# One table set for exponential and logarithm in the gates of a two-layer encoder kernel, and the lower bounds ahead of the first head

## The chip, the cores and the metric

The kernel runs on one core of a Trainium2 chip. The metric is device time in microseconds (us) for one execution, the median of several. The engines are TensorE (PE, with its weight loads as PEld), VectorE (DVE), ScalarE (ACT), GpSimd (POOL) and SyncE (SP), which issues transfers.

## The reference

Two layers of a bidirectional encoder trunk over 512 positions and 1024 channels, in float32. In each layer three branches start from one normalized input; their results are gated, summed, projected and added to the residual, and an MLP follows. The change touches branch A, a gated linear recurrence with four heads of 128 channels, run forward and backward. Its gates need an exponential and a logarithm:

```python
def hgrn2_gate(z, lb):
    zf = z.astype(jnp.float32)
    log_f = jnp.logaddexp(jnp.log(lb), jnp.log1p(-lb) + jax.nn.log_sigmoid(zf))
    key = (1.0 - lb) * jax.nn.sigmoid(-zf)
    return log_f, key
...
    p = jax.nn.softmax(lb_logits.astype(jnp.float32), axis=0)
    cum = jnp.cumsum(p, axis=0)
    lower = (cum - cum[0:1]).reshape(DEPTH, 2, A_HEADS, A_KDIM)
...
    merged = (gates[:, :, 0] * (y_a @ w_br[l, 0])
              + gates[:, :, 1] * (y_b @ w_br[l, 1])
              + gates[:, :, 2] * (y_c @ w_br[l, 2]))
```

`lower` is zero in layer 0, so only layer 1 needs the lower bounds' values. Branch B is a gated mixing with GELUs (computed with tanh), branch C an attention over a window of 128 positions with a softmax (exponentials), and `gates` are sigmoids (computed with tanh).

## The kernel before

Activations lie with channels on the 128 partitions and the 512 positions along the free dimension, or the other way round where a product asks for it. Matrix products are made exact enough by splitting each float32 operand into a high and a low part: ScalarE writes the high part of a weight chunk (L201), VectorE the low part (L202), and TensorE multiplies three of the four combinations (L206 to L208 and the like). Weights stream in 512 KB chunks on SyncE's queue.

A layer runs in stages. First come the token-major projections and the outer merge gates (`seven`, `on_gate`, which end in a tanh at L859 or L865). Then comes the stage of the three branches, which holds the change. Then the output projections and the MLP, where neither exponential nor logarithm is used. A second, smaller norm and spill of the residual connect the layers.

In the branch stage the program text runs: `a_ffb(0)` (two gate projections `f`, scaled into `z2` at L782, then `a_gates`), the query `q`, and `a_head` for head 0. Then in layer 0 `lower_bounds`. Then branch B's GELUs and mixing, the attention's keys and values, and by turns attention groups (`c_run`: `c_scores` with its Exp at L1022 and L1024, transposes `pT` at L1044 copied at L1045, outputs `po` copied to `yc` at L1057), the heads 1 to 3 (`head`), and columns of branch B's merge (`merge_b`: projection `gz`, tanh at L947, product `mg` at L953). A scheduler reorders all of this when the program is built: it takes, per engine, what is ready by a model of the durations, by the order of the text and by priorities (`hp`, `later`). The result is a fixed queue for each engine. `behind(mark)` makes every instruction in its block queue after `mark` on that engine.

`a_gates` computes on ScalarE the absolute value of `z2` (L582), its Exp (L583) and the Ln of one plus that (L584); in layer 1 a second round follows for the lower bound: Abs (L596), Exp (L598), Ln (L599). `a_head` makes from the cumulative sums `ex` many Exps: the factors `qt` and `kt` (L631, L634) for six block lengths, `key` (L648), `dec` (L676, L677), `kd` and `qd` (L682, L699). TensorE transposes `kd` (L685), ScalarE copies the transpose `kT` (L687), and TensorE multiplies it with the values (`stp`, L690).

[...] The program builder follows the finished ScalarE queue and puts an ACT_TABLE_LOAD before each activation whose function the loaded set lacks. These loads carry the line of the activation they precede. A load can also be asked for by the set's name.

## Time and profile before

| | |
|---|---|
| median of 3 executions | 1664.61 us (1662.26 to 1665.77) |
| the profiled execution | 1664.05 us |
| its span, first to last instruction | 1662.3 us |
| TensorE busy | 1640.4 us, 99% |
| VectorE busy | 1364.2 us, 82% |
| ScalarE busy | 1024.6 us, 62% |
| mean granted TensorE clock | 0.997 |

A row of a group names the source line, the engine, the operation, the result and its operands with their shapes, the count and, after the bar, busy us and the mean ns of one. A row of the timeline gives start and duration in us, and in brackets how long the engine had been idle and which instruction ended that. A row of waits names who waited for whom, with total us, times and longest. A row by stage gives the stage, its length, the busy time of PE, PEld, DVE, ACT and POOL with instruction counts, the granted clock of TensorE (1.00 is full), the share of time that the transfer engines are busy, and GB/s.

### The profile page before, as it was taken

The numbers are of one execution on the slowest core, as the hardware profiler recorded it, in microseconds if no ns is written. First come the engines' busy times: TensorE is split into PE (matmuls) and PEld (weight loads), VectorE is DVE, ScalarE is ACT, GpSimd is POOL, SyncE is SP. The second block draws the span as 40 slices with busy tenths as digits, with TensorE's granted clock in tenths as the row PEclk, the third lists the DMA queues.
The fourth block names the chain that finished last, engine by engine and source line by source line (L and its number), as shares of the span: only waits on it lengthen the run. The fifth ranks groups of instructions, "written<-read, shape, count | busy, mean of one in ns | idle before, by whom it ended". The sixth has DMA issues, their size and how long they took to land.

```text
span 1662.3 us, 24318 instructions
## 1 busy us (share of the span) xinstructions
PE 1640.4 (99%) x9137; PEld 1377.5 (83%) x9137; DVE 1364.2 (82%) x2183; ACT 1024.6 (62%) x1743; POOL 100.2 (6%) x165
## 2 busy tenths in 40 slices
PE   8999999999999999999999999999999999999998
PEld 6878887888888898989878888888888888989896
DVE  7887987877667989888989869888776589888987
ACT  7566578776246555646666665887862474646474
POOL 0011000000300000000010110000003000000001
PEclk9999999999999999999999999999999999999999
DMA  8243221322725233332423432212226243332311
GB/s 306 102 152 124 77 79 69 102 77 96 247 95 191 75 116 107 110 102 102 140 89 115 152 113 83 89 71 77 96 96 234 102 178 102 102 116 88 127 64 51
DMA packets 55589, 191.54 MB, mean 115 GB/s; under 512 B 7376, under 2 KB 7632, under 8 KB 55472
## 3 DMA queue, kind: packets, MB, share of 16 engines
q1 hardware_dynamic: 44352, 154.43, 27.0%
q0 software_dynamic: 10688, 35.00, 5.7%
q8 instruction: 72, 1.18, 0.3%
q10 hardware_dynamic: 432, 0.55, 0.1%
q14 instruction: 45, 0.37, 0.1%
HBM read 173.18 MB, written 16.78 MB: 114 GB/s over the span
## 4 chain that ended last, share of the span: by engine, by line
PE 66%; DVE 3%; ACT 2%; issue 1%; POOLq 0%; ACTq 0%; DVEq 0%
PE up L206 4%; PE up L207 4%; PE up L208 4%; PE dA L430 3%; PE dA L431 3%; PE dA L429 3%; PE us L517 2%; PE us L519 2%; PE us L518 2%; PE dC L430 2%; PE dC L429 2%; PE dC L431 2%; PE wo L249 2%; PE wo L250 2%; PE wo L248 2%; PE gA L429 1%
## 5 line engine op out<-in xcount | busy, mean ns | idle before, releaser
L201 ACT CAST wh<-wq 128x1024 fp32r<-128x1024 f32 x214 | 225.3, 1053 | 224.2 <-PE dA L430 61.3
L202 DVE TENSOR_TENSOR wl<-wq,wh 128x1024 fp32r<-128x1024 f32 x214 | 259.8, 1219 | 67.3 <-ACT wh L201 63.2
L201 ACT CAST wh<-wr 128x1024 fp32r<-128x1024 f32 x165 | 172.9, 1048 | 150.9 <-PE wo L249 23.4
L202 DVE TENSOR_TENSOR wl<-wr,wh 128x1024 fp32r<-128x1024 f32 x165 | 201.0, 1219 | 68.7 <-ACT wh L201 61.1
L208 PE MATMUL up<-xh,wl 128*128 128x512 f32 x320 | 124.7, 390 | 0.0
L207 PE MATMUL up<-xl,wh 128*128 128x512 f32 x320 | 124.7, 390 | 0.0
L206 PE MATMUL up<-xh,wh 128*128 128x512 f32 x320 | 124.5, 391 | 0.0
L430 PE MATMUL dA<-wh,sh 128*128 128x512 f32 x256 | 99.7, 389 | 0.0
L429 PE MATMUL dA<-wh,sh 128*128 128x512 f32 x256 | 98.4, 390 | 0.0
L431 PE MATMUL dA<-wl,sh 128*128 128x512 f32 x256 | 91.8, 389 | 0.0
L643 DVE TENSOR_TENSOR ex<-ex 128x512 f32<-128x512 f32 x112 | 74.7, 683 | 0.3
L206 PEld LDWEIGHTS up<-xh,wh 128*128 128x128 f32 x320 | 60.1, 188 | 12.6 <-ACT wh L201 0.2
L208 PEld LDWEIGHTS up<-xh,wl 128*128 128x128 f32 x320 | 60.1, 188 | 12.4
L207 PEld LDWEIGHTS up<-xl,wh 128*128 128x128 f32 x320 | 60.1, 188 | 12.2
L631 ACT ACTIVATE qt<-ex 128x512 f32<-128x512 f32 x56 | 38.0, 678 | 35.4 <-DVE ex L643 34.2
L429 PEld LDWEIGHTS dA<-wh,sh 128*128 128x128 f32 x256 | 48.0, 188 | 10.0
L431 PEld LDWEIGHTS dA<-wl,sh 128*128 128x128 f32 x256 | 48.1, 188 | 9.9
L430 PEld LDWEIGHTS dA<-wh,sh 128*128 128x128 f32 x256 | 48.1, 188 | 9.9
L518 PE MATMUL us<-xs,wh 128*128 128x256 f32 x192 | 54.1, 283 | 0.0
L517 PE MATMUL us<-xs,wh 128*128 128x256 f32 x192 | 54.1, 283 | 0.0
L519 PE MATMUL us<-xs,wl 128*128 128x256 f32 x192 | 53.3, 283 | 0.0
L207 PE MATMUL gz<-xl,wh 128*128 128x512 f32 x128 | 51.0, 399 | 0.0
(431 smaller groups left out, 4792.8 us busy)
## 6 DMA issues: line engine op xcount, KB each, us to landing
wr<-in_ws_dram SPq DMA_DIRECT2D x159, 512.0 KB, 3.5
wq<-in_ws_dram SPq DMA_DIRECT2D x124, 512.0 KB, 4.3
thd<-zt POOLq DMA_DIRECT2D x32, 256.0 KB, 2.5
gt<-thd POOLq DMA_DIRECT2D x32, 256.0 KB, 4.3
mgd<-mg POOLq DMA_DIRECT2D x16, 256.0 KB, 2.5
mB<-mgd POOLq DMA_DIRECT2D x16, 256.0 KB, 6.3
x<-in_xT_dram SPq DMA_DIRECT2D x8, 256.0 KB, 6.5
xt<-in_xt_dram SPq DMA_DIRECT2D x8, 256.0 KB, 5.8
```

Of the source, the lines that this page charges most:

```text
L201: nc.scalar.copy(hi, raw)
L202: nc.vector.tensor_tensor(lo, raw, hi.bitcast(F32), ALU.subtract)
L206: nc.tensor.matmul(pt, whi, xhi, start=first, stop=False)
L207: nc.tensor.matmul(pt, whi, xlo, start=False, stop=False)
L208: nc.tensor.matmul(pt, wlo, xhi, start=False, stop=last)
L429: nc.tensor.matmul(pt, xh[:, t], hi[:, c], start=start and k == 0, stop=False, skip_group_check=True)
L430: nc.tensor.matmul(pt, xl[:, t], hi[:, c], start=False, stop=False, skip_group_check=True)
L431: nc.tensor.matmul(pt, xh[:, t], lo[:, c], start=False, stop=k == 3, skip_group_check=True)
L517: nc.tensor.matmul(pt, hi[:, c], xh, start=n in (1, 2, 7) and k == 0, stop=False, skip_group_check=True)
L518: nc.tensor.matmul(pt, hi[:, c], xl, start=False, stop=False, skip_group_check=True)
L519: nc.tensor.matmul(pt, lo[:, c], xh, start=False, stop=k == 3, skip_group_check=True)
L643: nc.vector.tensor_tensor(o_ap, o_ap, ap_of(ex, i_, [[istep, 2]] + z), ALU.add)
```

## The change

Layer 0's call of `lower_bounds` moves ahead of the gates of its first head. In `lower_bounds` and in `a_gates` a load of the set `natural_log_exp_and_others` is asked for by name, queued on ScalarE behind the last Exp that comes before a Ln. Layer 0's head 0 is left without such a load of its own. The second logarithm of layer 1's gates (L599) is not touched.

```diff
@@ lower_bounds
         nc.scalar.activation(ea, ea, AF.Exp)
-        nc.scalar.activation(eb, eb, AF.Exp)
+        with behind(nc.scalar.activation(eb, eb, AF.Exp)):
+            nc.scalar.preload_act_table_set("natural_log_exp_and_others")
         s = SM("lb", 8)
@@ before a_gates
+    def log(t, mark):
+
+        if mark:
+            with behind(mark):
+                nc.scalar.preload_act_table_set("natural_log_exp_and_others")
+        nc.scalar.activation(t, t, AF.Ln, bias=onep_t[:, 0:1])
+
@@ a_gates
         nc.scalar.activation(e, z2, AF.Abs)
-        nc.scalar.activation(e, e, AF.Exp, scale=-1.0)
-        nc.scalar.activation(e, e, AF.Ln, bias=onep_t[:, 0:1])
+        mark = nc.scalar.activation(e, e, AF.Exp, scale=-1.0)
+        log(e, mark if l or h else None)
@@ trunk, start of the branch stage
         oa = []
+        if l == 0:
+            lbs = lower_bounds()
         g0 = a_ffb(0)
         q0 = evac(proj(xs, "q", l, "q", 0), "q", "q")
         oa.append(a_head(l, 0, g0, q0, vt))
-        if l == 0:
-            lbs = lower_bounds()
```

## The prediction

> **What bounds the kernel now.** I read the page first: engine totals, then the chain that ended last.

> ```profile
> span 1662.3 us, 24318 instructions
> PE 1640.4 (99%) x9137; PEld 1377.5 (83%) x9137; DVE 1364.2 (82%) x2183; ACT 1024.6 (62%) x1743; POOL 100.2 (6%) x165
> PE 66%; DVE 3%; ACT 2%; issue 1%; POOLq 0%; ACTq 0%; DVEq 0%
> ```

> TensorE (PE) is busy for 1640.4 of 1662.3 us and carries nearly all of the chain that a line is named for. ScalarE (ACT), the only engine whose work the change cuts, is busy 62%. So time taken off ScalarE counts only where PE stands still, or runs slowly, because of ScalarE. PE's whole idle time is 1662.3 - 1640.4 = 21.9 us: a ceiling over start, end and all stages.

> The second view is PE's waits, for the two stretches in which branch A's heads run: 140 to 420 us (layer 0), then 965 to 1250 us (layer 1).

> ```profile
> PE stp L690 <- ACT kT L687: 1.4, 1, 1.4
> PE po L1055 <- ACT pT L1045: 0.4, 1, 0.4
> PE pT L1044 <- ACT yc L1057: 0.4, 1, 0.4
> ...
> PE kT L685 <- ACT kd L682: 2.2, 1, 2.2
> PE pT L1044 <- DVE es L1026: 1.1, 1, 1.1
> PE pT L1044 <- ACT yc L1057: 0.6, 1, 0.6
> ```

> Columns: who waited for whom, total us, times, longest. These six waits, 6.1 us together, are all the standing still that a quicker ScalarE queue could remove inside the heads. Five name ScalarE, and the sixth (es) hangs on a ScalarE Exp.

> Third, how many table loads there are and which line they stand before (ScalarE's groups with shapes kept apart; count, busy us, mean ns):

> ```profile
> L584 ACT ACT_TABLE_LOAD x8 | 10.3, 1283 | 0.1
> L631 ACT ACT_TABLE_LOAD x4 | 5.1, 1283 | 1.1 <-DVE lbd L573 1.0
> L599 ACT ACT_TABLE_LOAD x4 | 5.1, 1283 | 0.1
> L676 ACT ACT_TABLE_LOAD x3 | 3.8, 1283 | 0.1
> L568 ACT ACT_TABLE_LOAD x2 | 2.6, 1283 | 0.0
> ...
> L947 ACT ACT_TABLE_LOAD x1 | 1.3, 1283 | 0.0
> ...
> L598 ACT ACT_TABLE_LOAD x1 | 1.3, 1283 | 0.0
> ```

> The view has 29 loads of 1.283 us; the rows left out are the one at the start and five before exponentials (L1022, L1024, L682). Fourteen stand before a logarithm (L584, L599, L568), fourteen before the next exponential or tanh after one. So today a logarithm evicts the exponential's tables and the next exponential brings them back.

> Fourth, ScalarE's timeline where PE waited: layer 0 head 2, then layer 1 head 1, then head 2.

> ```profile
> 285.43 1.28 ACT L682 ACT_TABLE_LOAD   x1
> 286.72 0.52 ACT L682 ACTIVATE kd<-ex 128x384 f32<-128x384 f32 x1
> ...
> 1049.91 1.28 ACT L676 ACT_TABLE_LOAD   x1
> 1051.31 0.51 ACT L682 ACTIVATE kd<-ex 128x384 f32<-128x384 f32 x1
> 1059.64 0.61 ACT L947 ACTIVATE gz<-gz 128x512 f32<-128x512 f32 x1
> 1061.87 1.28 ACT L599 ACT_TABLE_LOAD   x1
> 1064.84 1.28 ACT L1024 ACT_TABLE_LOAD   x1
> ...
> 1107.15 1.28 ACT L676 ACT_TABLE_LOAD   x1
> 1122.35 1.28 ACT L1024 ACT_TABLE_LOAD   x1
> ```

> In each, a load that brings the exponential back runs a microsecond or two before the instruction that PE waits for. PE's rows beside them, and the granted clock there:

> ```profile
> 288.07 0.94 PE L690 MATMUL stp<-vt,kT 128*128 128x128 f32 x6 [1.43 <-ACT kT L687]
> 1051.87 0.55 PE L685 MATMUL kT<-id_t,kd 128*128 128x128 f32 x3 [2.16 <-ACT kd L682]
> 1053.05 0.63 PE L207 MATMUL gz<-xl,wh 128*128 128x512 f32 x1
> ...
> 1125.59 0.52 PE L1044 MATMUL pT<-id_t,sc 128*128 128x128 f32 x3 [1.06 <-DVE es L1026]
> 286.00:292.00 6.00, 4.16 (x25) 3.00 (x24) 4.31 (x9) 5.90 (x14) 0.00 (x0) 1.00 0.00 0
> 1052.00:1057.00 5.00, 5.00 (x18) 4.19 (x19) 4.28 (x12) 4.94 (x16) 0.00 (x0) 0.66 0.30 108
> ```

> In the two last rows the figure behind the engines' busy times is the granted clock. After the 2.16 us wait it is 0.66 over 1052 to 1057, and a 128x512 matmul takes 0.63 us; after the 1.43 us wait it stays 1.00. The slow stretch costs 5 x (1 - 0.66) = 1.7 us on top of the wait. PE counts as busy in it, so the engine totals hide this.

> **The change part by part.**

> *Exponential and logarithm in one set.* In seven of the eight heads (all but layer 0 head 0) a load by name is issued behind the head's Exp (old L583) and ahead of its Ln (old L584); one more stands in `lower_bounds` ahead of its two Ln. The load costs what the one at L584 cost, 1.283 us, at the same place: nothing gained there. What goes is the load that brought the exponential back.

> What comes instead: does the named set hold tanh? The bounds are no load (it does) and one load per return to tanh. The nearest row is tanh's own load behind a logarithm:

> ```profile
> 262.45 1.28 ACT L947 ACT_TABLE_LOAD   x1
> DVE mg L953: 0.5, 1
> ```

> So tanh is missing from the set that is loaded for Ln today; I take it as missing from the named one too. [...] In the old order the merge gate's tanh (L947) follows each of heads 1, 2 and 3 in both layers: six returns. In layer 1 a tanh at 1059.64 lies between head 1's first Ln and its second (1061.87), and so in head 3; there the second Ln, which the change does not name a set for, and the Exp behind it load again: four. Loads after: 1 at the start + 8 by name + 6 + 4 = 19 against 29, or 10 x 1.283 = 12.8 us less on ScalarE.

> What a return to tanh costs PE: the one in the trace made VectorE's `mg` wait 0.5 us, once (last row), and no PE row waits for it. Between no cost and six full loads, 7.7 us, I take none, by that row; the cover is the next gate column's matmuls.

> *What PE gets.* (a) Layer 1 head 1: the load at 1049.91 is gone, so kd is 1.28 us earlier; head 0 before it loses three more loads (rows below) and hands over earlier. The 2.16 us wait closes and the slow clock with it: -2.2 and -1.7. (b) Layer 0 head 2: the load at 285.43 is gone: -1.3 of 1.43. (c) The `es` wait at 1125.59: the load at 1122.35 goes, as no tanh lies between head 2's two Ln: -1.1. (d) The two `yc` waits and the `pT` wait, 0.4 + 0.6 + 0.4, are all within a few us behind such a load: -1.4. Sum -7.7 us.

> [...]

> *Layer 1 head 0.* These loads lie on the chain that ended last (the first and the last of three), while PE has projections as cover (the stage's row below them):

> ```profile
> 994.52 1.28 ACT L598 ACT_TABLE_LOAD   x1
> ...
> 1001.34 1.28 ACT L631 ACT_TABLE_LOAD   x1
> 1020.00:1040.00 20.00, 20.00 (x143) 16.26 (x142) 19.91 (x34) 8.74 (x13) 0.00 (x0) 1.00 0.23 83
> ```

> All three go, 3.85 us. PE is busy for 20.00 of 20 us there, so nothing is gained at once; VectorE, 19.91 of 20, is next late. Counted at 0; it is what closes (a) wholly.

> *Lower bounds ahead of layer 0's first head.* In the old place their tiny instructions took four loads (259.59 to 269.77: both L568, L947 and the L631 that waits for `lbd`), with PE fully busy: no PE gain. In the new place they run as the first z arrives:

> ```profile
> 160.47 0.69 DVE L782 TENSOR_TENSOR z<-f,rb 128x512 f32<-128x512 f32 x1 [1.43 <-PE f L208]
> 165.89 1.29 DVE L587 SCALAR_TENSOR_TENSOR ex<-z,ga 128x512 f32<-128x512 f32 x2 [3.34 <-ACT ga L584]
> L566 DVE TENSOR_SCALAR lb<-lb x2: 157/159/161, 258.3 to 259.4; 128x8 f32<-128x8 f32 x2
> 140.00:160.00 20.00, 20.00 (x92) 16.63 (x91) 17.28 (x32) 11.35 (x16) 6.86 (x11) 1.00 0.58 201
> ```

> Some 17 VectorE instructions of 0.16 us (2.7 us) and four Exp or Ln of about 0.2 with the named load fit where VectorE has 20 - 17.28 and ScalarE 20 - 11.35 us free. Head 0's Ln then finds its set: two loads go there, and the 3.34 us wait shrinks by one of them. The block moves no DMA and passes nothing on SyncE's or GpSimd's queues; it is moved ahead of head 0's two gate projections and q, whose weight splits share ScalarE and VectorE. If that cover were gone, head 0 would start up to 2.7 + 1.3 + 0.8 = 4.8 us later; PE, 20.00 of 20 here, would feel what exceeds its own queue. Bounds 0 and +4.8; I take 0.

> *The order.* The matmul order and the ScalarE and VectorE queues are fixed when the program is built. Moving one block and adding eight instructions redraws the order of layer 0's heads and of all that follows. No row shows the new order. Bounds: from nothing to a repeat of the present stalls, 6.1 + 1.7 = 7.8 us; toward a gain they are already in the sum. I take +1.5, about one wait of (b)'s size, nearer the low end since waits of the six rows are mostly under 1.5.

> Sum: -7.7 + 1.5 = -6.2. The profiled execution took 1664.05 us (span 1662.3 and 1.75 around it), 0.56 under the median of 1664.61. So 1657.9 for a like execution and 1658.4 for the median: I say 1658.5.

> **The rivals.** A. *The wait moves* (no change): the closed waits bring PE sooner to VectorE, 19.91 of 20 us busy in the row above, and the same us are lost in waits for wl, ex or es. For it: VectorE is the fuller engine in the heads. Against: five of six waits name ScalarE. Then only (a)'s clock loss and little else is won: 1664 - 1.7 = 1662.3, range 1661.3 to 1667.9.

> B. *Slower: PE's redrawn queue puts kT or stp matmuls ahead of their kd.* Place: the 32 such groups (8 heads, two kT and two stp each). Price: the present case, 2.2 + 1.7 = 3.9 us each, because the clock falls. Point: two new ones cancel the gain of 7.7; with the third the time is 1664.6 - 7.7 + 11.7 = 1668.6, and four give 1672.5. For it: one of the 32 does so now and VectorE leaves it no slack. Against: exponentials without a load in front make every kd earlier.

> C. *The change does not do what it says*: the named set is not credited, and each Exp still gets its load. Then 8 named loads are added to 29 or replace those before Ln, and the time is 1664 to 1666. Nothing in the trace speaks for it.

> **How the numbers follow.** A measurement of this kernel tells about 0.2% (3.3 us) from no change; its three runs span 1662.26 to 1665.77. Forecast case 0.56 (own range 1655 to 1661.2; the lower end is all six waits and the clock loss gone, 1664.6 - 7.8 = 1656.8, and some 2 us of the 14 that PE idles elsewhere); A 0.23; B 0.17; C 0.04. Range 1654.5 to 1668: it leaves out most of B. Faster by over 0.2% is under 1661.3: 0.56. Same holds A and most of C: 0.27. Slower, over 1667.9: 0.17.

> **What the changed profile would show.** About 19 table loads, none before a head's factors (old L631), dec (L676) or kd (L682), and several before L947. No PE wait of 2 us for kd in layer 1, and a granted clock of 1.00 in every slice of 1000 to 1250 us. Lower bounds done before head 0's Abs. Wrong if the loads fall but PE's idle sum does not (A), if a slice of the heads shows a granted clock under 0.95 again (B), or if 29 or more loads remain (C).

## The result, and the profile after

The changed kernel takes 1652.17 us (median of 6 executions, 1651.11 to 1653.66), the kernel before 1664.53 us beside it (6 executions): a ratio of 0.9927, 95% interval 0.9916 to 0.9938. That is 12.4 us less, where 6 were forecast; the time lies 2.3 us under the stated range. A second set of 5 executions, beside 16 of the kernel before, gave 1651.74 against 1663.76, 0.9925 [0.9912, 0.9937]. The profiled execution took 1651.11 us, with a span of 1649.3.

First the page of the kernel after: span, engines, and the chain that ended last by engine.

```profile
span 1649.3 us, 24313 instructions
PE 1637.9 (99%) x9137; PEld 1378.3 (84%) x9137; DVE 1364.7 (83%) x2183; ACT 1014.5 (62%) x1735; POOL 100.0 (6%) x165
PE 97%; DVE 1%; DMA 1%; ACT 1%; issue 0%; POOLq 0%; DVEq 0%
```

TensorE (PE) does the same 9137 matmuls. Its idle time falls from 21.9 to 1649.3 - 1637.9 = 11.4 us, and ScalarE (ACT) is busy for 10.1 us less. Some 2 us of the idle time is the start's and not the change's: the wait for the first products, `bu`, is 2.7 us in that profile of before, 0.6 here, and 2.5 again in a second profile of the changed kernel, which idles for 14.0 us in all. Then PE's waits, over the whole kernel:

```profile
PE idle L165 <- DVE idle L162: 1.6, 1, 1.6
PE gA L429 <- ACT zt L867: 0.6, 1, 0.6
PE bu L206 <- ACT wh L256: 0.6, 1, 0.6
PE tA L429 <- DVE xr L473: 0.4, 1, 0.4
PE wo L248 <- DVE mB L1142: 0.3, 1, 0.3
PE gA L431 <- DVE wl L202: 0.2, 1, 0.2
```

All six waits of the heads are gone, and no new one stands in their place. Two slices of the heads' stages, layer 1 and layer 0 (length, busy PE, PEld, DVE, ACT and POOL, then the granted clock), say the same: PE is busy for the whole slice, at full clock, where before it waited 2.2 us and then ran at a granted clock of 0.66 over 1052 to 1057, and waited 1.4 us.

```profile
1040.00:1060.00 20.00, 20.00 (x134) 16.99 (x133) 15.65 (x42) 18.37 (x37) 0.54 (x1) 1.00 0.20 66
280.00:300.00 20.00, 20.00 (x145) 17.19 (x142) 14.92 (x39) 13.21 (x30) 2.19 (x4) 1.00 0.31 107
```

ScalarE's groups of table loads:

```profile
L582 ACT ACT_TABLE_LOAD x7 | 9.0, 1283 | 0.1
L954 ACT ACT_TABLE_LOAD x7 | 9.0, 1283 | 0.1
L607 ACT ACT_TABLE_LOAD x3 | 3.8, 1283 | 0.1
L1029 ACT ACT_TABLE_LOAD x2 | 2.6, 1283 | 0.0
L159 ACT ACT_TABLE_LOAD x1 | 1.3, 1283 | 1.2 <-PEq L1385 1.2
L553 ACT ACT_TABLE_LOAD x1 | 1.3, 1283 | 0.0
```

There are 21 loads against 29: eight by name (L582, L553), seven returns to the merge gate's tanh (L954), three for the second logarithm (L607), two for an exponential after one of those (L1029), and the one at the start (L159). None stands before the factors, `dec` or `kd`. ScalarE's timeline at layer 1 head 1 shows it:

```profile
1037.12 1.28 ACT L582 ACT_TABLE_LOAD   x1
1038.42 1.15 ACT L583 ACTIVATE ga<-ga,onep_t 128x1024 f32<-128x1024 f32 x1
1039.47 1.03 ACT L201 CAST wh<-wr 128x1024 fp32r<-128x1024 f32 x1
1040.41 0.20 ACT L684 ACTIVATE ms<-ex 128x2 f32<-128x2 f32 x1
1040.52 0.51 ACT L690 ACTIVATE kd<-ex 128x384 f32<-128x384 f32 x1
...
1050.41 1.28 ACT L954 ACT_TABLE_LOAD   x1
```

The load by name stands where the logarithm's stood; behind the weight cast, `dec` and `kd` (now L684 and L690) follow at once, and the tanh's load comes 10 us later.

### The profile page after: what moved, and what is told of

It is laid out like the page before. It is cut to its first block, busy times and chain, and to the rows that moved or that the text cites. A ratio compares the mean times of both kernels' runs of the same rounds, so it can differ in the third digit from the quotient of the medians.

```text
span 1649.3 us, 24313 instructions
## 1 busy us (share of the span) xinstructions
PE 1637.9 (99%) x9137; PEld 1378.3 (84%) x9137; DVE 1364.7 (83%) x2183; ACT 1014.5 (62%) x1735; POOL 100.0 (6%) x165
## 4 chain that ended last, share of the span: by engine, by line
PE 97%; DVE 1%; DMA 1%; ACT 1%; issue 0%; POOLq 0%; DVEq 0%
PE up L206 4%; PE up L208 4%; PE up L207 4%; PE dA L429 3%; PE dA L430 3%; PE dA L431 3%; PE us L517 2%; PE us L519 2%; PE us L518 2%; PE at L623 2%; PE f L206 2%; PE f L208 2%; PE gz L208 2%; PE f L207 2%; PE gz L206 2%; PE gz L207 2%
## 5 line engine op out<-in xcount | busy, mean ns | idle before, releaser
L207 PE MATMUL up<-xl,wh 128*128 128x512 f32 x320 | 124.7, 390 | 0.0
L208 PE MATMUL up<-xh,wl 128*128 128x512 f32 x320 | 124.7, 390 | 0.0
L208 PEld LDWEIGHTS up<-xh,wl 128*128 128x128 f32 x320 | 60.1, 188 | 12.4
L207 PEld LDWEIGHTS up<-xl,wh 128*128 128x128 f32 x320 | 60.1, 188 | 12.2
L206 PE MATMUL f<-xh,wh 128*128 128x512 f32 x128 | 50.7, 396 | 0.0
```

Source lines behind the costliest of these rows:

```text
L206: nc.tensor.matmul(pt, whi, xhi, start=first, stop=False)
L207: nc.tensor.matmul(pt, whi, xlo, start=False, stop=False)
L208: nc.tensor.matmul(pt, wlo, xhi, start=False, stop=last)
```

## Where the 12 us lie

The traces can be cut at the same matmuls: the heads from the first product of gate `f` to the first of `yA` (branch A's merge), the output projection of layer 0 from the first `wo` to the first `up` (the MLP's first product), the end from layer 1's first `up`. Lengths in us by stage and profile (the last column is the median with its own comparison to before):

| kernel | loads | heads, layer 0 | heads, layer 1 | `wo`, layer 0 | end | ratio to before |
|---|---|---|---|---|---|---|
| before, 4 profiles | 29 | 280.5 to 280.6 | 280.8 to 281.8 | 48.8 | 332.2 to 332.4 | 1 |
| after, 2 profiles | 21 | 277.1 | 275.3 | 47.3 | 331.5, 331.7 | 0.9925 [0.9912, 0.9937] |
| e6, no logarithm, old queues | 1 | 277.6 | 275.0 | 48.8 | 332.0 | 0.9934 [0.9922, 0.9947] |
| e7, none in layer 1, old queues | 13 | 280.6 | 275.0 | 48.8 | 332.0 | 0.9957 [0.9943, 0.9971] |
| e3, new queues, set natural_log | 33 | 280.9, 281.2 | 277.2 | 47.3 | 331.9, 332.1 | 0.9972 [0.9961, 0.9982] |
| e1, move alone | 27 | 280.8 (see e1) | 280.3 | 47.3 | 332.0 | 0.9981 [0.9972, 0.9991] |
| e2, loads by name, no move | 28 | 279.4 | 275.3 | 48.8 | 332.0 | 0.9964 [0.9951, 0.9978] |
| e4, second Ln by name too | 23 | 277.1 | 276.2 | 47.3 | 332.5 | 0.9941 [0.9929, 0.9954] |
| e5, no tanh, new queues | 10 | 277.1 | 275.2 | 47.3 | 331.6 | 0.9928 [0.9916, 0.9941] |

Before to after, by the means of the profiles: heads -3.5 and -5.9, `wo` -1.5, end -0.7, together -11.5 where the medians differ by 12.0. The spans of these six profiles differ by 12.9; the rest lies in the start and in layer 0's MLP, where profiles of one kernel differ among themselves by more than that.

## The experiments

**The changed kernel again (e0_after_again).** No edit.

> The changed kernel once more, 21 table loads, as the reference for the kernels that run beside it. Both theories: 1652 (1651 to 1654). If the 1.5 us that the changed kernel's profile was ahead at 40 us, before any changed instruction, belongs to that one execution and not to the change, this profile's first product of the token stage starts anywhere from 26.5 to 28 us.

Measured: 1651.74 us. The start differs between two profiles of one kernel: layer 0's first `f` comes at 147.4 and at 148.5. The lead that the first profile had at 40 us was that execution's.

**The same queues with a set that holds no exponential (e3_log_only_set).**

```diff
-            nc.scalar.preload_act_table_set("natural_log_exp_and_others")
+            nc.scalar.preload_act_table_set("natural_log")
```

(in both places)

> The changed kernel with the set natural_log asked for by name instead of natural_log_exp_and_others. The queues of TensorE, ScalarE and VectorE are those of the changed kernel, instruction for instruction; only the loads differ: 33 against 21, since each exponential behind a logarithm brings its own set back. Theory 'loads' (PE's waits came from the exponential's reloads): 1661 to 1667, with PE waits of 1 us and more for kd, kT or es in the heads. Theory 'order' (the redrawn queues are better whatever is loaded): 1652 to 1655.

Measured: 1659.61 us, ratio 0.9972, with 33 loads. Every engine's queue is that of the changed kernel apart from the loads, so the loads alone are worth 7.9 us in this order. PE's waits name the heads again:

```profile
PE kT L693 <- ACT kd L690: 1.8, 1, 1.8
PE q L206 <- DVE z L790: 0.9, 1, 0.9
PE kT L693 <- ACT at L677: 0.4, 1, 0.4
PE at L623 <- DVE key L657: 0.4, 1, 0.4
PE stp L698 <- ACT kT L695: 0.3, 1, 0.3
```

and its timeline shows the reload in front of the `kd` that PE waits for:

```profile
1109.46 1.28 ACT L684 ACT_TABLE_LOAD   x1
1110.76 0.21 ACT L684 ACTIVATE ms<-ex 128x2 f32<-128x2 f32 x1
1110.87 0.51 ACT L690 ACTIVATE kd<-ex 128x384 f32<-128x384 f32 x1
```

Theory "loads" holds in its mechanism. Its 1661 was too high: with more loads than before the kernel is still 4.2 us faster than before, so theory "order" has its part. The two parts do not simply add: the new order is worth 4.2 us with an exponential's reloads in it, and 1.5 us without them (the changed kernel against e6, the next run).

**The old queues without logarithms (e6_no_log_old_order).** Leaves out every Ln: each is an Abs (a Copy in the lower bounds) of the same shape.

```diff
-        nc.scalar.activation(e, e, AF.Ln, bias=onep_t[:, 0:1])
+        nc.scalar.activation(e, e, AF.Abs, bias=pad_t[:, 0:1], scale=1e-3)
...
-            nc.scalar.activation(g, g, AF.Ln)
+            nc.scalar.activation(g, g, AF.Copy, scale=-1.0)
```

> The kernel before with its logarithms left out: each Ln is an Abs (or, in the lower bounds, a Copy) of the same shape and with the same kinds of operands. The queues are those of the kernel before; 1 load against 29. Theory 'loads': the six PE waits of the heads (6.1 us) and the slow clock (1.7 us) go: 1656.7, between 1654 and 1659. Theory 'order': 1662 to 1665, with waits for kd, kT and yc still there.

Measured: 1653.28 us, 10.5 under before, more than expected. PE's queue is that of the kernel before, so the two can be laid side by side matmul by matmul. In the heads e6's lead grows in steps: 1.59 us at `stp` (288.07), 0.58 and 0.52 at `pT` and `po` (290.93, 337.29), 2.23 at `kT` (1051.87) and 1.4 over the seven slow matmuls behind it, 0.72 and 1.13 at the two `pT` (1110.83, 1125.59). These are the six waits and the slow clock and nothing else above 0.15 us: 8.2 in sum. Each step is some 0.1 us more than the idle time in the row. No wait is left in the heads. Those for `mgl`, the low part that the first `wo` products need, stayed; the two rows above them belong to the token stages:

```profile
...
PE tA L429 <- DVE xr L473: 0.8, 1, 0.8
PE gA L429 <- ACT zt L859: 0.6, 1, 0.6
PE wo L249 <- DVE mgl L257: 0.4, 2, 0.3
```

**Layer 1's logarithms left out alone (e7_no_log_layer1).** Same edit, in layer 1's gates only.

> The kernel before with layer 1's logarithms left out (each Ln an Abs of the same shape and kinds of operands); layer 0's and those of the lower bounds stay. The queues are those of the kernel before; 13 loads against 29. Theory 'each PE wait is priced by itself': layer 0's head stage stays at 280.5 us with its three waits, layer 1's falls from 280.8 to 275.0, and the median is 5.8 us under before, plus some 0.5 for a clock that falls less often: about 1657.5. Rival 'the waits only move': what is closed in layer 1 comes back later in that layer, and the gain is under 3 us.

Measured: 1658.07 us against 1665.46 beside it, ratio 0.9957 [0.9943, 0.9971]. Layer 0's heads stay at 280.6 with their three waits, layer 1's fall to 275.0, as in e6. The waits add up; none moved on within the heads.

**The move alone (e1_move_only).** The call of `lower_bounds` ahead of head 0, no load by name.

> The kernel before with only the lower bounds moved ahead of layer 0's first head, no load by name: 27 loads, queues drawn anew. Theory 'loads': 1661 to 1667, as the reloads in front of kd, dec and the factors stay. Theory 'order': if the move is what drew the better order, 1652 to 1656.

Measured: 1660.88 us, ratio 0.9981 [0.9972, 0.9991]: 2.9 us, just under what was expected of "loads". The heads keep waits, some in other places. The three rows that name `kd`, `yc` and `es`:

```profile
PE kT L685 <- ACT kd L682: 2.7, 2, 2.2
PE pT L1043 <- ACT yc L1056: 1.6, 2, 1.0
PE pT L1043 <- DVE es L1025: 1.1, 1, 1.1
```

Its gain is in three places: the `wo` stage (47.3 against 48.8), the clock, which did not fall behind this 2.2 us wait (mean granted clock 0.999 in this profile, 0.997 in that of before), and layer 0's heads. The table hides the last one, because eight products of branch C (`yC`) stand ahead of the first `yA` here and behind it in all other kernels. From the first `f` to the first `wo` layer 0 takes 306.1 us against 307.8 to 307.9 before. The waits in PE's rows explain 0.3 us of that (2.0 against 2.3); the rest was not traced.

**The loads alone (e2_loads_only).** The changed kernel with `lower_bounds` called behind head 0, as before.

> The changed kernel with the lower bounds at their old place behind head 0: 28 loads, since their logarithms fall among head 1's exponentials and merge gates. Theory 'what counts is what PE waits for': layer 1 keeps the whole gain (-5.5 us), layer 0 keeps what its reloads in front of kd gave unless the lower bounds' eight loads make PE wait: 1652 to 1657. Rival 'the move carries the change': 1660 or more.

Measured: 1657.55 us, ratio 0.9964 [0.9951, 0.9978]. Layer 1 has the whole gain, layer 0 a third of it, and the `wo` waits are back. Two waits in layer 0's heads are new, the larger of 2.0 us:

```profile
PE f L206 <- DVE z L790: 2.0, 1, 2.0
PE q L206 <- DVE z L790: 0.3, 1, 0.3
```

So the move brings more than the `wo` stage: without it layer 0's heads lose 2.3 of the 3.5 us again, for these waits. They name VectorE, but what VectorE had waited for is again a table load. Ahead of this `z` its queue has `lbr`, a step of the lower bounds, which waits for ScalarE's second small logarithm and the load in front of it:

```profile
265.36 1.28 ACT L569 ACT_TABLE_LOAD   x1
266.89 0.17 DVE L571 TENSOR_TENSOR lbr<-lb,lb 128x8 f32<-128x8 f32 x1 [0.81 <-ACT lb L569]
```

Before that VectorE had been idle for 1.1 us for the first such logarithm and 1.7 us for a factor `qt` behind an exponential's reload.

**The tanh left out (e5_no_tanh).** The merge gate's and the output gate's tanh are Abs.

```diff
-                nc.scalar.activation(z, z, AF.Tanh, scale=0.5)
+                nc.scalar.activation(z, z, AF.Abs, scale=0.5)
```

(and the like for `th`)

> The changed kernel with the tanh of branch B's merge gate and of branch A's output gate left out (each an Abs of the same shape, which every set holds): the queues are the same, 10 loads against 21. Theory 'what counts is what PE waits for': 1651.7, within 1.5 us, since PE waits 0.02 us in the heads of the changed kernel. Rival 'every load on ScalarE has a price': 11 loads of 1.28 us less, so some 1640 to 1645.

Measured: 1651.97 us, ratio 0.9928 [0.9916, 0.9941], against 0.9925 for the changed kernel. Eleven loads fewer, 14 us of ScalarE, and no change that the run can tell. That every set holds Abs is shown only for the sets that were loaded: none of the 10 loads here stands before an Abs, and none of the 29 in before, where an Abs at 993.12 (L596) follows the logarithm at 989.41 (L584). The heads take 277.1 and 275.2 us, as in the changed kernel. PE waits behind none of these loads, and so they are free here. The returns to tanh that the prediction priced at nothing cost nothing that this run can tell.

**The second logarithm by name too (e4_second_named).**

```diff
-            nc.scalar.activation(z2, z2, AF.Exp, scale=-1.0)
-            nc.scalar.activation(z2, z2, AF.Ln, bias=onep_t[:, 0:1])
+            log(z2, nc.scalar.activation(z2, z2, AF.Exp, scale=-1.0))
```

> The changed kernel with the set asked for by name ahead of layer 1's second logarithm too: 23 loads, queues drawn anew. Theory 'what counts is what PE waits for': no gain is left in the heads, so 1651 to 1655, the upper part if the new order has a wait of its own. Rival 'the second Ln's reloads still cost': 1646 to 1650.

Measured: 1654.3 us, ratio 0.9941 [0.9929, 0.9954], within the expectation and no better than the changed kernel; layer 1's heads are 0.8 us longer in the order that it draws. No kernel that was run is clearly faster than the changed one.

**Further profiles of the kernel before and of e3 (e0_before_again, e8_before_look2, e8_before_look3, e8_log_only_look2).** No edits.

> The kernel before once more, for its profile. If its start is slower than the changed kernel's by nature, the first gate projection (149 us in the first profile, 147.4 and 148.5 in the changed kernel's two) is again near 149 and the end stage again over 332 us; if that was one execution's accident, they lie among the others (147.4 to 148.5; 331.5 to 332.0). Both theories: the six waits of the heads are there again, as the queues are the same.

> A further profile of the kernel before. Theory 'a PE wait makes the clock fall in some executions only': the six waits repeat within 0.2 us, but the slow stretch behind them is not at the same waits in each execution; lost clock in the heads between 0 and 3.5 us, and the time follows it. Rival 'the clock falls behind the one wait of 2.2 us and nowhere else': 1.7 us lost in layer 1's heads, none in layer 0's, in every profile.

> As the profile before it: the two theories differ in whether the lost clock in the heads is the same in each execution.

> A further profile of the changed kernel with the set natural_log. Its first profile had a slow stretch behind a 1.56 us wait at the start of layer 1's token stage and none behind a 1.82 us wait for kd. Theory 'some executions only': the slow stretch is elsewhere or missing. Rival 'by the length or place of the wait': at the same wait again.

Measured: 1665.01, 1665.32 and 1664.46 us for the kernel before, 1659.5 for e3. The first `f` comes at 149.8, 148.5 and 147.9 us, so the start is the execution's. In the heads each profile of before lost 1.7 us of clock, behind the `kd` wait of layer 1, and none elsewhere: there the rival, "behind that wait alone", holds. But that wait itself is not the same each time: 2.2, 2.2, 2.4 and 3.1 us. The largest, from the last of the profiles:

```profile
1052.12 0.55 PE L685 MATMUL kT<-id_t,kd 128*128 128x128 f32 x3 [3.10 <-ACT kd L682]
```

For e3 the slow stretch of its first profile was missing in the second, where the `tA` wait ahead of it was 0.7 us instead of 1.56; the 1.82 us wait for `kd` had none in both. So the length of a wait alone does not tell whether the clock falls behind it: 1.56 us with a fall, 1.82 without (the last section has more).

## Why the prediction was wrong

*That a logarithm evicts the exponential's tables and that PE waits behind the reload*: right. e3 (33 loads, 1659.61 us, against 21 and 1651.74 on the new queues) and e6 (1 load, 1653.28 us, against 29 and 1663.76 on the old ones) show it from both sides, on fixed queues.

One term of the sum came true by luck. For (c), the `es` wait, the prediction held that head 2's second logarithm would need no load, as no tanh lies between its two logarithms. In the new order one does (1110.55), and both the second logarithm and the exponential behind it load again:

```profile
1111.85 1.28 ACT L607 ACT_TABLE_LOAD   x1
...
1116.38 1.28 ACT L1029 ACT_TABLE_LOAD   x1
```

The wait is gone all the same, because PE's new queue has `gz` and `yB` products to do there from 1115.7 to 1120.7. e3, with the same queues, has no `es` wait either.

*The sum of the six waits and the clock, -7.7*: right in kind, somewhat small. Point by point in e6 it is 8.2, since the steps there are some 0.1 us longer than the idle times in the rows (1.59 against 1.43 at `stp`); against the mean of four profiles of before, the heads of the changed kernel give 9.3, of which some 0.3 is the `kd` wait, which was at its smallest in the profile that the prediction rests on. Steps under 0.15 us, not traced one by one, make up most of the rest. The clock term, put at 1.7, is 1.4 to 1.6 of this.

*The redrawn order, +1.5*: this is the step that failed. I allowed only for waits that a new order brings and held that anything gained was already in the sum. Measured, the new order costs the heads nothing (552.5 us for both layers against 552.6 in e6, the old order without loads), and it gives 1.5 us in a stage that the prediction left out, the output projection. Every kernel with the move has 47.3 us there, every one without it 48.8. VectorE's timeline around the first `wo` of the kernel before:

```profile
455.62 0.68 DVE L1146 TENSOR_TENSOR mC<-mC,gt 128x512 f32<-128x512 f32 x1
456.22 1.27 DVE L1145 SCALAR_TENSOR_TENSOR gt<-gt,yA 128x512 f32<-128x512 f32 x2
457.41 0.68 DVE L257 TENSOR_TENSOR mgl<-mB,mgh 128x512 fp32r<-128x512 f32 x1
```

and of the kernel after:

```profile
447.53 1.28 DVE L1142 TENSOR_TENSOR mB<-mB,mT 128x512 f32<-128x512 f32 x2
448.89 0.69 DVE L257 TENSOR_TENSOR mgl<-mB,mgh 128x512 fp32r<-128x512 f32 x1
449.50 0.68 DVE L1152 SCALAR_TENSOR_TENSOR gt<-gt,yA 128x512 f32<-128x512 f32 x1
```

Before, three gate products and sums run ahead of the first low part `mgl`, which is ready 1.4 us after PE's first `wo` at 456.7; after, `mgl` starts 2.8 us before the first `wo` at 451.7. Laid side by side, the two kernels' `wo` stages part by 1.5 us within their first 6.5 us, at the two waits for `mgl` (0.4 us in PE's row above) and the steps beside them, where PE's order differs as well. That the move brings this is shown by the kernels with and without it; that it acts through VectorE's order is read from these timelines and was not tested alone. So the term was mis-sized by 3.0 us, and its sign was wrong. Of the 5.8 us between the forecast of 6.2 and the 12.0 measured, these are the largest part; the heads' sum adds 1.6 and the end 0.7.

*The end, not in the prediction*, gives 0.7. Of this 0.5 lies behind PE's last matmul, in the last norm and the transfer out: 7.9 to 8.0 us pass from there to the end of the span in the four profiles of before, 7.4 in both of after, and 7.4 to 8.3 in the experiments. The last matmul of before and of after:

```profile
1653.99 0.39 PE L431 MATMUL dA<-wl,sh 128*128 128x512 f32 x1
```

```profile
1641.55 0.39 PE L431 MATMUL dA<-wl,sh 128*128 128x512 f32 x1
```

The granted clock falls to 0.50 near the end of both profiles, but only after that matmul (at 1657.0 and at 1645.5), so this fall costs PE nothing. Whether the change has any hand in the 0.7 is open.

*Layer 1 head 0, counted at 0, and the returns to tanh, counted at 0*: right; e6 shows the first, as its lead has no step there, and e5 the second. *Lower bounds ahead of head 0, counted at 0*: right in cost, though the last of their logarithms starts at 160.8, behind head 0's Abs and just ahead of its Exp. *19 loads*: 21, with seven returns to tanh instead of six and five loads around the second logarithms instead of four, without effect. The seven loads before L954 also show that the named set lacks tanh, as was assumed. *Rivals*: A (the wait moves) is refuted by e7, where closed waits stayed closed though VectorE's queue was that of before, where it is busy for 19.91 of 20 us at 1020. B did not come: no wait for `kd` was drawn. Its price rested on a clock that falls behind each such wait, which e1 (2.2 us) and e3 (1.82 us) do not show. C is refuted by the loads.

*The range* had at its lower end all six waits and the slow clock gone, 7.8 us, and some 2 us of PE's idle time elsewhere, in no named stage. The heads gave 9.3, and `wo` and the end together 2.2; that is most of the 2.3 us by which it ended too high.

## What to carry to other kernels

Where one engine is the bound, price a ScalarE table load by the wait that the bound engine has behind it, row by row: here 28 loads gone from the old queues bought little more than what six waits and the slow clock behind one of them cost, and eleven loads gone from the new queues bought nothing. Ask for a set that holds both functions by name when a plain logarithm would bring one that lacks the exponential (21 loads here, 33 with `natural_log`), and move small logarithms out of the stretches where exponentials are urgent. A change to any instruction redraws a scheduled program far downstream, so take the order's part as open to both sides and look for waits in the stages behind. Where a wait names an engine, ask what that engine had waited for: in e2 it was a table load once more.

## What was not expected of the hardware

```profile
832.55 0.50 PE L429 MATMUL tA<-wh,xh 128*128 128x512 f32 x1 [1.56 <-DVE xr L473]
```

and two slices of the same profile, with the granted clock third from the end:

```profile
833.00:838.00 5.00, 5.00 (x19) 3.90 (x18) 4.51 (x10) 2.30 (x8) 1.09 (x3) 0.66 0.46 158
1109.00:1114.00 5.00, 3.18 (x51) 2.70 (x46) 4.12 (x9) 4.97 (x14) 0.00 (x0) 1.00 0.32 107
```

The first slice is the stage behind that wait; the second holds the 1.82 us wait for `kd`, at full clock. Waits of 1.6 us (a profile of before), 2.0 (e2) and 2.2 (e1) had no fall either, and the waits of 2.2 to 3.1 in before had one each time.

The clock's own records in the traces tell more. The fall behind `kd` in the first profile of before lasts 3.413 us, and in two profiles the falls start whole multiples of that apart: at 1052.857 and 1657.016 in the first profile of before, 177.0 times 3.413, and at 833.540 and 1656.152 in the first of e3, 241.0 times. Two windows of that length, one of before that ended in a fall, and one of e1 that holds 1.4 of its 2.2 us wait and did not:

```profile
1049.44:1052.86 3.41, 1.26 (x17) 1.12 (x14) 2.57 (x5) 3.38 (x8) 0.00 (x0) 1.00 0.15 47
1044.64:1048.05 3.41, 2.00 (x37) 1.43 (x35) 3.40 (x7) 3.38 (x4) 0.00 (x0) 1.00 0.13 53
```

PE is busy for 37% of the first and 59% of the second; the rest of e1's wait fell into the next window. With the whole run cut into such windows, laid so that the falls start with one, and leaving out windows in which the clock was already down, the two of the first profile of before in which PE was least busy, 0.78 us (23%, from 1653.60) and 1.26 us (37%, from 1049.44), were each followed by a fall; the next two, 1.65 us (48%, from 22.03) and 1.98 us (58%, from 284.86, where the 1.43 us wait lies), were not. In e3 the window ahead of the fall at 833.540 holds the whole 1.56 us wait, so PE was busy for some 54% of it, more than in the window with 48% that had no fall. In the profile of after, the one window with PE wholly idle, from 1642.13, was followed by the only fall, and the next, with PE busy for 83% (from 106.13), was not. So the falls went with the idle time within one window more than with the length of a wait, and e1's wait, which lay in two, passed without one; a limit does not show, and no run varied this alone.

Beside the 1.283 us of a table load ScalarE's rows show next to no idle time: in the profile of after the activation before ends within 0.02 us of the load's start, and the next begins within 0.02 us of its end (1036.04 + 1.06, then 1037.12; 1037.12 + 1.28, then 1038.42), and the eight loads at L584 of before have 0.1 us of idle time ahead of them in all.
